# Down-projection steps behind half products, and exponentials in pieces, in a one-core encoder layer

## The chip, the cores and the metric

The kernel is one launch on one core of a Trainium2 chip. The metric is the time of the launch on the device in microseconds (us). Three runs of the kernel before took 2942.41, 2954.04 and 2954.80 us; the median is 2954.04 us. The names of the engines are those of the profile: PE is the matrix engine, PEld its weight loads, DVE the vector engine, ACT the engine for activation functions, POOL the general one, SP the one that issues all DMAs here.

## What is computed

One encoder layer on 2048 tokens of width 1024 in fp32: three mixers side by side (A: an attention that keeps 256 keys for each query, chosen by an index score; B: gated linear attention in chunks of 64; C: attention in a window), an output projection, and a gated feed-forward part (FFN) with 2816 inner columns.

```python
h = rms_norm(x, norm_mix[l])
p = h @ w_in[l]
out_a = dsa_mixer(q_a, c_kv, q_idx, k_idx, w_idx, kv_norm[l], w_uk[l], w_uv[l], rel_bias)
out_b = gla_mixer(q_b, k_b, v_b, g_lr, r_b, w_gate2[l], b_gate[l], gla_norm[l])
out_c = swa_mixer(q_c, k_c, v_c, sinks[l], rel_bias)
x = x + jnp.concatenate([out_a, out_b, out_c], axis=-1) @ w_out[l]
h = rms_norm(x, norm_ffn[l])
x = x + (jax.nn.silu(h @ w_ffn_gate[l]) * (h @ w_ffn_up[l])) @ w_ffn_down[l]
return rms_norm(x, final_norm)
```

In mixer A a block of 128 queries scores all earlier keys, keeps 256 (`lax.top_k`), adds a bias to their logits, takes a softmax and sums the values.

## The kernel before

Activations lie transposed, 128 channels on the partitions and 512 tokens (a group) along a row; there are four groups. Every dense product is made of two parts for each operand (`hi`, and `lo`, the rest), as three matmuls of 512 columns for each 128 rows of the contraction: a product with 8 such rows is 24 matmuls, and half of it (`FINE = 4` rows) is 12.

Two threads of work run at the same time on the one core, written as Python generators. The dense thread, `dense`, goes through the input projections (`pass1`), mixers B and C (`pass2`), and then the output projection and FFN (`ffn`) of groups 0 and 1. The other thread, `dsa`, goes through the 16 query blocks of mixer A: `select` of a block runs beside `attend` of the block ahead of it. `merge` takes a step of the thread that is behind by its share: each `yield` gives the cost of the step just written, in units of its author's, and the totals stand at the `merge` call (`FFN1`, `select_cost`, `attend_cost`, `SPEED`). The steps come out as one program, and a scheduler then moves single instructions ahead where their inputs and buffers allow, so that the final order on each engine is that of the `order` listings below. After both threads are done, `last` runs the output projection and FFN of groups 2 and 3 alone (`ffn` with two halves).

`select` finds the 256th largest score by bisection: 32 probes over the whole row, in turns on ACT (L935) and DVE (L937), each of which gives a count, and two short DVE instructions between them (L960, L962) that set the next threshold. Then a scan and masks (L983 to L990) make the mask `mk`. `attend` computes logits by strips on PE (L1030 to L1032), masks them and takes the extreme on DVE (L1034), takes one exponential per head over the whole row on ACT (L1038), turns 128x128 pieces on PE (L1047), copies them out of PSUM on ACT (L1049) and sums values on PE (L1057).

In `ffn`, `gate_up(f)` makes one of 22 inner tiles: the gate product, a tanh on ACT (L277) and a DVE instruction (L278), the up product, a DVE instruction (L283, tile `u`), and its split into `fh` and `fl` (ACT L116, POOL L119). `down(fs, ...)` adds two inner tiles to the output: eight steps (one for each output tile `oc`), each of six matmuls (L299 to L301) and an add to `x2` on DVE (L302; the profile writes `x`). In groups 0 and 1 the order is `gate_up(f)`, then all eight steps of `down([f - 2, f - 1])`, then `gate_up(f + 1)`. Products and steps take their PSUM bank in turn from the three of `mf`. `norm_scale` (L202) and `finish` (L324, L326) close a group.

Weights come 128x512 at a time into `w`, a ring of `N_W` buffers. Group 0 loads each from the input (`raw`), splits it on ACT (L116) and POOL (L119) and stores the two parts; later groups load the stored parts (L131). The rings of `w` and of `fh`/`fl` before, and the order of the inner loop:

```python
N_RAW, N_W, N_ACT = 3, 5, 3
...
for f in range(0, NF, 2):
    yield from gate_up(f)
    if f and n_act < 4:
        yield from down([f - 2, f - 1], steps)
    yield from gate_up(f + 1)
```

Of the kernel before, what the change touches and what calls it, by code (L numbers as in the profile page):

```python
# [1 line left out]

# [17 lines left out]
P = 128  # L20
# [57 lines left out]

N_RAW, N_W, N_ACT = 3, 5, 3
A_RAW, A_W = 3, 5  # L80
# [4 lines left out]
def hybrid_encoder_kernel(ctx, tc, xT, w_in, w_out, w_g, w_u, w_d, vec, wuk, wuv, wg2,  # L85
# [73 lines left out]

    def ffn(groups, pools, ps_f, ps_n, n_raw, n_w, n_act, n_lead, before):  # L160

# [7 lines left out]

        def product(ps, w, act, ks=range(KC), first=True, last=True):  # L170

            for k in ks:
                hi, lo = w[k // 4]
                a, b = (t[:, (k % 4) * P:(k % 4 + 1) * P] for t in (hi, lo))
                T.matmul(ps, a, act[k][0], start=(first and k == ks[0]), stop=False)  # L175
                T.matmul(ps, b, act[k][0], start=False, stop=False)  # L176
                T.matmul(ps, a, act[k][1], start=False, stop=(last and k == ks[-1]))  # L177
                if k % FINE == FINE - 1 and k < ks[-1]:
                    yield 0.65 * FINE


# [38 lines left out]
        def normed(i):  # L220

            hs = halves[i]
            norm_scale(hs)
            h2.append([])
            for k in range(KC):
                h2[i].append(operand(i, k))
                hi, lo = h2[i][k]
                hf = fr.tile([P, 512], F32, tag="m", bufs=3, name="hf")
                V.scalar_tensor_tensor(out=hf, in0=x2[:, k, hs], scalar=vc[:, V_FFN + k:V_FFN + k + 1],
                                       in1=rs[:, hs], op0=ALU.mult, op1=ALU.mult)  # L230
                A.copy(hi, hf)  # L231
                (V if k % 2 else Q).tensor_sub(lo, hf, hi.bitcast(F32))
                yield 0.4
# [31 lines left out]

        def gate_up(f):
            ah = ft.tile([P, W], F32R, tag="fh", bufs=n_act, name="fh")
# [4 lines left out]
            for i, hs in enumerate(halves):  # L272
                pg = ps_f()
                yield from product(pg, wg_, h2[i])

                s = ft.tile([P, 512], F32, tag="s", bufs=2, name="s")
                A.activation(s, pg, AF.Tanh, scale=0.5)  # L277
                V.scalar_tensor_tensor(out=s, in0=s, scalar=1.0, in1=pg, op0=ALU.add, op1=ALU.mult)  # L278
                yield 5.2 - 0.65 * (KC - FINE)
                pu = ps_f()  # L280
                yield from product(pu, wu_, h2[i])
                u = ft.tile([P, 512], F32, tag="u", bufs=2, name="u")
                V.scalar_tensor_tensor(out=u, in0=s, scalar=0.5, in1=pu, op0=ALU.mult, op1=ALU.mult)  # L283
                split(u, ah[:, hs], al[:, hs])
                yield 5.2 - 0.65 * (KC - FINE)

        def down(fs, parts, last=False):

            n, ws = len(fs), {}
            for i2, hs in parts:  # L290
                if i2 not in ws:
                    ws[i2] = [load_w(w_d, f, i2) for f in fs]
                for oc in range(i2 * 4, i2 * 4 + 4):
                    os_ = slice((oc % 4) * P, (oc % 4 + 1) * P)
                    ps = ps_f()[:, 0:hs.stop - hs.start]
                    for j, f in enumerate(fs):
# [41 lines left out]
        for f in range(0, NF, 2):  # L338
            yield from gate_up(f)
            if f and n_act < 4:  # L340
                yield from down([f - 2, f - 1], steps)
            yield from gate_up(f + 1)
            if f and n_act >= 4:
                yield from down([f - 2, f - 1], steps)
        yield from down([NF - 2, NF - 1], tail, True)
# [5 lines left out]
    with ExitStack() as mx:  # L351
# [648 lines left out]
        def attend(qb, res):  # L1000
# [15 lines left out]
            far = nk - nw  # L1016
            sl = strips(far) + [(far, nw)]
            den = sp.tile([P, 4], F32, tag="dena", name="dena")
            po = ps_o()

            def logits(hd):
# [5 lines left out]
                for si, (k0, w) in enumerate(sl):  # L1027
# [9 lines left out]
                    yield 0.9 * w / 512.0  # L1037
                A.activation(lg[:, 0:nk], lg[:, 0:nk], AF.Exp, scale=-1.0, bias=least[:, si:si + 1],  # L1038
                             accum_out=den[:, hd:hd + 1])

# [22 lines left out]
            for h2 in (0, 2):  # L1063
                yield from logits(h2)
                yield from logits(h2 + 1)
                for k4 in range(0, qb + 1, 4):
                    nxt = [turned(h2, k4)]
                    if wait:
                        summed(*wait)
                    nxt.append(turned(h2 + 1, k4))  # L1070
                    wait = nxt
                    yield 2.0 * nxt[0][2] / 4.0
            V.reciprocal(den, den)

# [3 lines left out]
            V.tensor_copy(dT, pt[0:4, 0:P])  # L1078
            summed(*wait)
            pb = ps_tr()  # L1080
            for hd in range(4):
# [10 lines left out]
        def attend_cost(qb):  # L1092
            return (qb + 1) * (0.9 + 1.0) + 1.5

# [24 lines left out]
        def dense():  # L1119
# [9 lines left out]
            with ExitStack() as f1:  # L1129
# [5 lines left out]
                for g in range(2):  # L1135
                    while len(attended) < 4 * g + 4:
                        yield None
                    end = yield from ffn([g], pools, lambda: mf.tile([P, 512], F32, tag="mf", name="mf"), ps_tr,
                                         N_RAW, N_W, N_ACT, 2, end)
# [5 lines left out]
    with ExitStack() as f2:  # L1145
# [6 lines left out]
        def last():  # L1152
            end = yield from ffn([2, 3], pools, lambda: pp.tile([P, 512], F32, tag="pf", name="pf"),
                                 lambda: pr.tile([P, 512], F32, tag="pm", name="pm"), 3, 9, 4, 6, iter(()))
# [93 lines left out]
```

## Time and profile before

| what | before |
|---|---|
| median of 3 runs | 2954.04 us |
| profiled execution, its own time | 2950.48 us |
| its span, first to last instruction | 2948.7 us |
| outside the span | 1.8 us |
| PE busy | 2761.6 us, 94% of the span |
| DVE, ACT, POOL busy | 57%, 40%, 20% |
| mean granted TensorE clock | 0.973 |
| chain that ended last | PE 59%, DVE 19%, ACT 8%, issue 7%, DMA 4% |

The table is read like this: PE is the engine that is busy nearly all of the time, so what counts is where it stands still and where it runs at the lower clock. A busy PE is not PE at its peak: a matmul of 512 columns is shown as 0.39 us long, while the next one starts 0.23 us after it. The profiled execution is 3.6 us faster than the median and 8.1 us slower than the fastest run.

The stages by time: projections and mixers B and C to about 970 us, the FFN of group 0 to about 1540 us, that of group 1 to 2083 us, the end of mixer A to 2103 us, and groups 2 and 3 to the end.

### The profile page before, as it was taken

The page shows a single profiled execution, that of the slowest core. Times are in us where ns is not written, and L with a number is a line of the kernel's source. Part 1 is how long each engine was busy: PE and PEld are TensorE (multiplying, and loading weights), DVE is VectorE, ACT ScalarE, POOL GpSimd, SP SyncE. Part 2 cuts the span into 40 slices and gives each one's busy share as a digit, 9 for nine tenths or more (in the row PEclk, how much of TensorE's full clock was granted, in tenths as well). Part 3 has the DMA queues.
Part 4 walks back from the last instruction along what each step waited for, and adds up shares of the span by engine and source line. Part 5 has one row for each costly group of instructions (what it writes and reads, how often), then busy time and mean ns, then how long its engine had stood idle before and what let it go on. Part 6 is the DMA issues. An engine that isn't in the chain of part 4 may idle for free.

```text
span 2948.7 us, 36635 instructions
## 1 busy us (share of the span) xinstructions
PE 2761.6 (94%) x13372; PEld 2171.4 (74%) x13372; DVE 1677.2 (57%) x3567; ACT 1181.1 (40%) x2061; POOL 582.8 (20%) x497
## 2 busy tenths in 40 slices
PE   7898999999999899999989999999899999999997
PEld 5666767676776767777767777777677888888886
DVE  3787887788767867475576673673342222222226
ACT  4655664665546655354553431441341000000004
POOL 3113420010100544444431100001111000000002
PEclk9998999999999989999999999999999999999998
DMA  7665534243332756666655444444572323323222
GB/s 248 193 190 191 183 122 142 92 149 106 103 128 78 268 179 229 227 214 225 226 187 193 142 150 143 137 152 147 188 249 87 108 92 100 100 86 107 93 93 72
DMA packets 179300, 451.12 MB, mean 153 GB/s; under 512 B 18632, under 2 KB 50288, under 8 KB 179120
## 3 DMA queue, kind: packets, MB, share of 16 engines
q1 hardware_dynamic: 179120, 448.78, 46.1%
q8 instruction: 105, 1.72, 0.2%
q14 instruction: 75, 0.61, 0.1%
HBM read 325.88 MB, written 122.83 MB: 152 GB/s over the span
## 4 chain that ended last, share of the span: by engine, by line
PE 59%; DVE 19%; ACT 8%; issue 7%; DMA 4%; POOL 2%; SPq 0%; DVEq 0%; ACTq 0%; POOLq 0%
PE pf L175 6%; PE pf L177 6%; PE pf L176 6%; DVE jd L937 6%; ACT jd L935 4%; PE mf L177 4%; PE mf L175 4%; PE mf L176 4%; PE pf L301 2%; PE pf L300 2%; PE pf L299 2%; PE mm L507 2%; PE mm L506 2%; PE mm L508 2%; PE mf L299 2%
## 5 line engine op out<-in xcount | busy, mean ns | idle before, releaser
L935 ACT ACTIVATE jd<-x,c 128x384 bf16<-128x384 f32 (+13 forms) x224 | 292.8, 1307 | 288.5 <-DVE c L962 228.7
L177 PE MATMUL mf<-al,w 128*128 128x512 f32 x832 | 329.1, 396 | 8.3 <-DVE al L212 4.1
L175 PE MATMUL mf<-ah,w 128*128 128x512 f32 x832 | 331.5, 399 | 3.7 <-ACT ah L231 2.8
L937 DVE TENSOR_SCALAR_CACHE_REDUCE jd<-x,c 128x384 bf16<-128x384 f32 (+13 forms) x224 | 330.9, 1477 | 6.5 <-DVE c L946 0.5
L175 PE MATMUL pf<-ah,w 128*128 128x512 f32 x832 | 325.1, 391 | 6.2 <-DMA w<-w 4.5
L119 POOL TENSOR_TENSOR w<-raw,w 128x512 fp32r<-128x512 f32 x192 | 260.0, 1362 | 341.4 <-ACT w L116 297.0
L176 PE MATMUL mf<-ah,w 128*128 128x512 f32 x832 | 327.4, 395 | 0.0
L177 PE MATMUL pf<-al,w 128*128 128x512 f32 x832 | 324.8, 391 | 1.3 <-POOL al L212 0.6
L176 PE MATMUL pf<-ah,w 128*128 128x512 f32 x832 | 325.3, 391 | 0.0
L119 POOL TENSOR_TENSOR fl<-u,fh 128x512 fp32r<-128x512 f32 x88 | 114.2, 1298 | 948.5 <-ACT fh L116 948.4
L506 PE MATMUL mm<-hh,w 128*128 128x512 f32 x576 | 241.3, 419 | 4.3 <-issue 2.0
L507 PE MATMUL mm<-hh,w 128*128 128x512 f32 x576 | 232.2, 403 | 0.6 <-POOL w L119 0.6
L508 PE MATMUL mm<-hl,w 128*128 128x512 f32 x576 | 230.9, 401 | 0.0
L177 PEld LDWEIGHTS mf<-al,w 128*128 128x128 f32 x832 | 158.5, 191 | 46.4 <-DVE al L212 4.5
L175 PEld LDWEIGHTS mf<-ah,w 128*128 128x128 f32 x832 | 159.0, 191 | 38.4 <-ACT ah L231 3.4
L175 PEld LDWEIGHTS pf<-ah,w 128*128 128x128 f32 x832 | 156.9, 189 | 39.9 <-DMA w<-w 4.9
L302 DVE TENSOR_TENSOR x<-x,pf 128x512 f32<-128x512 f32 (+1 forms) x184 | 121.9, 663 | 110.3 <-PE pf L301 110.0
L177 PEld LDWEIGHTS pf<-al,w 128*128 128x128 f32 x832 | 156.8, 188 | 35.9 <-POOL al L212 1.0
L176 PEld LDWEIGHTS mf<-ah,w 128*128 128x128 f32 x832 | 158.5, 190 | 31.7
L176 PEld LDWEIGHTS pf<-ah,w 128*128 128x128 f32 x832 | 156.8, 188 | 32.8 <-issue 0.5
L116 ACT CAST fh<-u 128x512 fp32r<-128x512 f32 x88 | 54.6, 620 | 308.1 <-DVE u L283 307.6
L299 PE MATMUL mf<-fh,w 128*128 128x512 f32 x352 | 147.0, 418 | 32.7 <-DVE x L302 17.3
(256 smaller groups left out, 5473.1 us busy)
## 6 DMA issues: line engine op xcount, KB each, us to landing
w<-w SPq DMA_DIRECT2D x636, 512.0 KB, 3.5
xk<-in_xT_dram SPq DMA_DIRECT2D x64, 256.0 KB, 3.3
raw<-in_w_in_dram SPq DMA_DIRECT2D x44, 256.0 KB, 3.7
raw<-in_w_g_dram SPq DMA_DIRECT2D x44, 256.0 KB, 3.7
raw<-in_w_u_dram SPq DMA_DIRECT2D x44, 256.0 KB, 3.9
raw<-in_w_d_dram SPq DMA_DIRECT2D x44, 256.0 KB, 4.3
m<-mixT SPq DMA_DIRECT2D x32, 256.0 KB, 3.1
x<-in_xT_dram SPq DMA_DIRECT2D x32, 256.0 KB, 4.6
```

The costliest lines, as they stand in the source:

```text
L119: Q.tensor_sub(lo, src, hi.bitcast(F32))
L175: T.matmul(ps, a, act[k][0], start=(first and k == ks[0]), stop=False)
L176: T.matmul(ps, b, act[k][0], start=False, stop=False)
L177: T.matmul(ps, a, act[k][1], start=False, stop=(last and k == ks[-1]))
L299: T.matmul(ps, hi[:, os_], ah[:, hs], start=(j == 0), stop=False)
L300: T.matmul(ps, lo[:, os_], ah[:, hs], start=False, stop=False)
L302: V.tensor_add(x2[:, oc, hs], x2[:, oc, hs], ps)
L506: T.matmul(ps, a, hh, start=(k == 0), stop=False)
L507: T.matmul(ps, b, hh, start=False, stop=False)
L508: T.matmul(ps, a, hl, start=False, stop=(k == KC - 1))
L935: A.activation(jd, xs, AF.Sign, scale=-1.0, bias=c[:, 0:1], accum_out=cnt)
L937: V.tensor_scalar(out=jd, in0=xs, scalar1=c[:, 0:1], scalar2=0.0, op0=ALU.is_ge, op1=ALU.add, accum_out=cnt)
```

## The change

- The down steps of groups 0 and 1 are no longer in one run of eight. `product` takes a generator `beside` and takes one step of it after its first half; `gate_up` takes one after each product. So a step of six matmuls stands behind each half product of twelve, and the eight steps of two tiles are spread over two `gate_up`.
- These steps have a PSUM bank of their own (`md`, one buffer); gate and up products keep two (`mf`). Groups 2 and 3 are as before.
- The ring of `w` has 7 buffers instead of 5, that of `fh` and `fl` 4 instead of 3.
- The exponential of a head is taken in pieces of 512 columns, each with its own sum in `dens`; the sums are added on DVE before the reciprocal.
- `attend` yields at five more kinds of places (5.0 units in all for a block), so that dense work may be written there, and `attend_cost` grows by 5.0. `normed` yields 3.0 before the norm.

```diff
-N_RAW, N_W, N_ACT = 3, 5, 3
+N_RAW, N_W, N_ACT = 3, 7, 4
...
                 if k % FINE == FINE - 1 and k < ks[-1]:
                     yield 0.65 * FINE
+                    yield from islice(beside, 1)
...
             hs = halves[i]
+            yield 3.0
             norm_scale(hs)
...
-                yield from product(pg, wg_, h2[i])
+                yield from product(pg, wg_, h2[i], beside=beside)
...
                 yield 5.2 - 0.65 * (KC - FINE)
+                yield from islice(beside, 1)
...
-                    ps = ps_f()[:, 0:hs.stop - hs.start]
+                    ps = ps_d()[:, 0:hs.stop - hs.start]
...
-            yield from gate_up(f)
-            if f and n_act < 4:
-                yield from down([f - 2, f - 1], steps)
-            yield from gate_up(f + 1)
-            if f and n_act >= 4:
-                yield from down([f - 2, f - 1], steps)
+            last_two = down([f - 2, f - 1], steps) if f else iter(())
+            for f_ in (f, f + 1):
+                yield from gate_up(f_, last_two if nh == 1 else iter(()))
+            yield from last_two
...
+            n4 = (nk + 511) // 512
+            dens = sp.tile([P, 4, 4], F32, tag="dens", name="dens")
...
-                A.activation(lg[:, 0:nk], lg[:, 0:nk], AF.Exp, scale=-1.0, bias=least[:, si:si + 1],
-                             accum_out=den[:, hd:hd + 1])
+                for j, k0 in enumerate(range(0, nk, 512)):
+                    e = lg[:, k0:min(k0 + 512, nk)]
+                    A.activation(e, e, AF.Exp, scale=-1.0, bias=least[:, si:si + 1],
+                                 accum_out=dens[:, hd, j:j + 1])
+                yield 0.5
...
+                    if k4 == 0:
+                        yield 1.0
...
-            V.reciprocal(den, den)
+            if n4 > 1:
+                V.tensor_reduce(out=den, in_=dens[:, :, 0:n4], axis=AX.X, op=ALU.add)
+                V.reciprocal(den, den)
+            else:
+                V.reciprocal(den, dens[:, :, 0])
+            yield 0.5
...
             summed(*wait)
+            yield 0.5
...
-            return (qb + 1) * (0.9 + 1.0) + 1.5
+            return (qb + 1) * (0.9 + 1.0) + 6.5
...
-                mf = f1.enter_context(tc.tile_pool(name="mf", bufs=3, space=PSUM))
...
-                    end = yield from ffn([g], pools, lambda: mf.tile([P, 512], F32, tag="mf", name="mf"), ps_tr,
+                    end = yield from ffn([g], pools, lambda: mf.tile([P, 512], F32, tag="mf", bufs=2, name="mf"),
+                                         lambda: mf.tile([P, 512], F32, tag="md", bufs=1, name="md"), ps_tr,
```

The change in the order of instructions is shown at three places. First DVE in the FFN of group 1, beside the probes of the last query block (2048 columns). `jd,cnt<-x,c` is a probe, `up` and `c` set the next threshold, `s` and `u` take a gate and an up product out of PSUM, and `x_...<-x_...,mf` is the add of a down step. Before:

```order
L960 TENSOR_SCALAR up<-cnt,nth,ps_16671 128x1
L962 TENSOR_SCALAR c<-c,st,up 128x1
L937 TENSOR_SCALAR jd,cnt<-x,c 128x2048
L283 SCALAR_TENSOR_TENSOR u<-s,mf 128x512
L960 TENSOR_SCALAR up<-cnt,kp,ps_16671 128x1
L962 TENSOR_SCALAR c<-c,st,up 128x1
L302 TENSOR_TENSOR x_14013<-x_14013,mf 128x512 x2
L960 TENSOR_SCALAR up<-cnt,nth,ps_16671 128x1
L962 TENSOR_SCALAR c<-c,st,up 128x1
L937 TENSOR_SCALAR jd,cnt<-x,c 128x2048
L302 TENSOR_TENSOR x_14013<-x_14013,mf 128x512 x2
```

The same place now, with the line numbers of the changed file:

```order
L941 TENSOR_SCALAR jd,cnt<-x,c 128x2048
L308 TENSOR_TENSOR x_13931<-x_13931,md 128x512
L964 TENSOR_SCALAR up<-cnt,kp,ps_17170 128x1
L966 TENSOR_SCALAR c<-c,st,up 128x1
L964 TENSOR_SCALAR up<-cnt,nth,ps_17170 128x1
L966 TENSOR_SCALAR c<-c,st,up 128x1
L308 TENSOR_TENSOR x_13931<-x_13931,md 128x512
L941 TENSOR_SCALAR jd,cnt<-x,c 128x2048
L964 TENSOR_SCALAR up<-cnt,kp,ps_17170 128x1
L966 TENSOR_SCALAR c<-c,st,up 128x1
L288 SCALAR_TENSOR_TENSOR u<-s,mf 128x512
```

Adds in pairs behind a probe have become single adds, about one for each DVE probe, each with a bank `md` behind it.

Second ACT at the end of the `attend` that runs beside the last `select` (`fh` is a split, `s` a tanh, `pT` a copy out of PSUM). Before:

```order
L976 ACTIVATE jd,cnt<-x,ntt,sg 128x2048
L116 CAST fh<-u 128x512
L1038 ACTIVATE big,dena<-big,least 128x1920
L277 ACTIVATE s<-mf 128x512
L1049 COPY pT<-tr 128x512 x2
L116 CAST fh<-u 128x512
```

The same stretch of the block ahead of it, now:

```order
L980 ACTIVATE jd,cnt<-x,ntt,sg 128x1920
L281 ACTIVATE s<-mf 128x512
L1046 ACTIVATE big,dens<-big,least 128x512 x3
L1046 ACTIVATE big,dens<-big,least 128x256
L1058 COPY pT<-tr 128x512
L117 CAST fh<-u 128x512
```

One exponential has become four in a row.

Third DVE at the end of group 1, where mixer A ends too (`dT`, `ma` and `ll` are short steps of `attend`, `big,least<-sc,...` is a strip of logits, `rs` the sum of squares of the last norm, L326 and L332 its `finish`). Before:

```order
L1078 COPY dT<-tr 4x128
L1087 TENSOR_TENSOR ma<-o,bs 128x256
L302 TENSOR_TENSOR x_14013<-x_14013,mf 128x512 x8
L1013 SCALAR_TENSOR_TENSOR ll<-sc,lh 128x512
L1034 ISA big,least<-sc,mk 128x512
L1034 ISA least 128x1
L1034 ISA big,least<-sc,mk,least 128x512
L1034 ISA least 128x1
L278 SCALAR_TENSOR_TENSOR s<-s,mf 128x512
```

Now:

```order
L308 TENSOR_TENSOR x_13931<-x_13931,md 128x512
L199 TENSOR_TENSOR rs<-rs,sq 128x512
L332 SCALAR_TENSOR_TENSOR x_13931<-x_13931,vc,rs 128x512 x5
L1094 COPY dT<-tr 4x128
L1104 TENSOR_TENSOR ma<-o,bs 128x256
L1017 SCALAR_TENSOR_TENSOR ll<-sc,lh 128x512
L1040 ISA big,least<-sc,mk 128x512
L1040 ISA least 128x1
```

The `attend` of the last block stood beside the last products and steps of group 1 (84 matmuls come on PE after its first one); now it stands behind the end of the group, with no dense work beside it.

## Rows read from the trace of the kernel before

**Rows 1.** Windows by stage: us, PE, PEld, DVE, ACT, POOL busy, clock, DMA.

```profile
970.00:1540.00 570.00, 527.34 (x2527) 418.24 (x2525) 368.07 (x693) 299.54 (x461) 257.31 (x199) 0.96 0.64 219
1540.00:2040.00 500.00, 469.99 (x2287) 377.42 (x2288) 299.53 (x530) 174.16 (x232) 43.38 (x40) 0.97 0.48 155
2104.00:2949.00 845.00, 816.32 (x3610) 673.57 (x3608) 251.79 (x363) 119.30 (x192) 94.44 (x74) 0.99 0.35 116
```

**Rows 2.** Waits of PE from 0 to 2104 us: total, times, longest.

```profile
PE mf L299 <- DVE x L302: 17.3, 11, 3.4
...
PE mf L299 <- DVE u L283: 12.0, 6, 4.5
...
PE tr L1082 <- DVE dT L1078: 5.4, 3, 3.1
...
PE mf L299 <- ACT fh L116: 2.7, 1, 2.7
```

**Rows 3.** PE groups, 970 to 2104 us: busy, mean ns, idle before, releaser.

```profile
L1047 PE MATMUL tr<-cs,big 128*128 128x128 f32 x344 | 56.1, 286 | 17.2 <-ACT big L1038 15.8 <-ACT rs L148 1.3
L1057 PE MATMUL o<-pT,cv 128*64 128x128 f32 x688 | 53.3, 285 | 9.0 <-ACT pT L1049 9.0
```

**Rows 4.** Timeline of PE at 1902 us, a down step's start.

```profile
1902.50 0.39 PE L300 MATMUL mf<-fh,w 128*128 128x512 f32 x1
1902.73 0.39 PE L301 MATMUL mf<-fl,w 128*128 128x512 f32 x1
1907.65 0.79 PE L299 MATMUL mf<-fh,w 128*128 128x512 f32 x1 [4.54 <-DVE u L283]
```

**Rows 5.** Timeline of DVE in the same stretch.

```profile
1898.90 2.34 DVE L937 TENSOR_SCALAR_CACHE_REDUCE jd<-x,c 128x2048 bf16<-128x2048 f32 x1
...
1904.03 0.27 DVE L960 TENSOR_SCALAR up<-cnt,nth,ps 128x1 f32<-128x1 f32 x1 [2.16 <-ACT jd L935]
...
1904.64 2.35 DVE L937 TENSOR_SCALAR_CACHE_REDUCE jd<-x,c 128x2048 bf16<-128x2048 f32 x1
...
1906.91 0.68 DVE L283 SCALAR_TENSOR_TENSOR u<-s,mf 128x512 f32<-128x512 f32 x1
```

**Rows 6.** Windows of 20 us with a low granted clock (column before the last two).

```profile
1720.00:1740.00 20.00, 15.09 (x52) 11.21 (x51) 15.48 (x32) 6.96 (x8) 1.26 (x1) 0.83 0.32 100
...
1900.00:1920.00 20.00, 15.46 (x71) 12.19 (x70) 14.56 (x25) 7.86 (x9) 1.29 (x1) 0.83 0.28 90
```

**Rows 7.** Line L302: ns min/median/max, first and last start.

```profile
L302 DVE TENSOR_TENSOR x<-x,mf x176: 655/684/691, 1090.9 to 2080.5; 128x512 f32<-128x512 f32 x176
```

**Rows 8.** Line L131, 1600 to 2040 us: reloads of weights, issue to landing.

```profile
DMA to landing us min/median/max: 3.3/3.5/5.3
```

**Rows 9.** Groups of 970 to 1540 us: the two splits of a weight.

```profile
L119 POOL TENSOR_TENSOR w<-raw,w 128x512 fp32r<-128x512 f32 x146 | 198.1, 1366 | 243.1 <-ACT w L116 208.5 <-DMA w<-w 7.0 <-DMA raw<-in_w_g_dram 6.3
...
L116 ACT CAST w<-raw 128x512 fp32r<-128x512 f32 x145 | 87.8, 615 | 88.2 <-PE mf L177 37.2 <-PE mf L301 19.0 <-issue 13.6
```

**Rows 10.** ACT groups by form: the exponentials' total and mean ns.

```profile
L1038 ACT ACTIVATION_READ_ACCUMULATOR big<-big,least 128x1 f32 x64 | 11.9, 186 | 0.0
...
L1038 ACT ACTIVATE big<-big,least 128x1920 f32<-128x1920 f32 x4 | 7.6, 1900 | 9.4 <-DVE least L1034 9.4
...
L1038 ACT ACTIVATE big<-big,least 128x512 f32<-128x512 f32 x4 | 2.9, 720 | 4.2 <-DVE least L1034 4.2
```

**Rows 11.** Timeline of DVE at the last scan, and at the close of group 1.

```profile
1981.97 4.42 DVE L985 TENSOR_TENSOR_SCAN x<-ones,mk 128x2048 f32<-128x2048 f32 x1
...
2088.88 6.54 DVE L326 SCALAR_TENSOR_TENSOR x<-x,vc,rs 128x512 f32<-128x512 f32 x5
```

**Rows 12.** Windows of 20 us at the end of mixer A.

```profile
2060.00:2080.00 20.00, 19.45 (x130) 15.22 (x130) 9.80 (x18) 12.81 (x21) 1.92 (x2) 1.00 0.00 1
2080.00:2100.00 20.00, 17.46 (x124) 12.68 (x122) 13.29 (x26) 12.32 (x16) 4.62 (x3) 0.91 0.40 145
```

**Rows 13.** Waits of PE, 2040 to 2200 us: the longest one.

```profile
PE pf L175 <- DMA w<-w: 4.5, 1, 4.5
```

More of the change, by code (lines that the diff above doesn't have):

```diff
@@ L1 @@
 from contextlib import ExitStack
+from itertools import islice
 import numpy as np
@@ L157, in sigmoid, with ffn @@
         A.activation(dst, dst, AF.Exp)
-    def ffn(groups, pools, ps_f, ps_n, n_raw, n_w, n_act, n_lead, before):
+    def ffn(groups, pools, ps_f, ps_d, ps_n, n_raw, n_w, n_act, n_lead, before):
         fx, ft, fh, fl, fo, fs, fr = pools
@@ L168, in load_w, with product @@
             return load_halves((src.tensor.name, f, c), src[f][:, c * 512:(c + 1) * 512], fr, n_raw, fh, n_w)
-        def product(ps, w, act, ks=range(KC), first=True, last=True):
+        def product(ps, w, act, ks=range(KC), first=True, last=True, beside=iter(())):
             for k in ks:
@@ L264, in ffn, with gate_up @@
             yield from normed(i)
-        def gate_up(f):
+        def gate_up(f, beside=iter(())):
             ah = ft.tile([P, W], F32R, tag="fh", bufs=n_act, name="fh")
@@ L279, in gate_up @@
                 yield 5.2 - 0.65 * (KC - FINE)
+                yield from islice(beside, 1)
                 pu = ps_f()
-                yield from product(pu, wu_, h2[i])
+                yield from product(pu, wu_, h2[i], beside=beside)
                 u = ft.tile([P, 512], F32, tag="u", bufs=2, name="u")
@@ L285, in gate_up @@
                 yield 5.2 - 0.65 * (KC - FINE)
+                yield from islice(beside, 1)
         def down(fs, parts, last=False):
@@ L1152, in last @@
         def last():
-            end = yield from ffn([2, 3], pools, lambda: pp.tile([P, 512], F32, tag="pf", name="pf"),
+            ps_f = lambda: pp.tile([P, 512], F32, tag="pf", name="pf")
+            end = yield from ffn([2, 3], pools, ps_f, ps_f,
                                  lambda: pr.tile([P, 512], F32, tag="pm", name="pm"), 3, 9, 4, 6, iter(()))
```

## The prediction

> **What bounds the kernel now.** First I read the windows by stage, to see where PE, the engine that is busy 94% of the span, stands still. In the last 845 us (groups 2 and 3 alone) PE is busy 816 of 845 us at a clock of 0.99, and the change leaves this stage as it is [rows 1]. What it moves lies ahead of 2104 us, most of all in the two FFN stages from 970 to 2040 us: there PE is idle 43 and 30 us, and the clock of 0.96 and 0.97 stands for 23 and 15 us more at full speed (570 x 0.04, 500 x 0.03) [rows 1]. The waits of PE say what the idle time is: 32.0 us before the first matmul of a down step (L299), which waits for its PSUM bank: 17.3 us for the adds of earlier steps, 12.0 us for `u`, which still reads a product's bank, and 2.7 us for `fh` [rows 2]; 15.8 us before transposes that wait for an exponential, and 9.0 us before value sums that wait for a copy by ACT [rows 3]. Then I read one such wait on both engines. PE has finished a step and stands from 1903 to 1907.65 for `u` [rows 4]. DVE had nothing long of its own to do for `u`: 0.68 us. But `u` was queued behind a threshold update that waited 2.16 us for a probe on ACT, and behind the next probe of 2.35 us [rows 5]. Behind such waits the clock falls: the window from 1900 to 1920 us has 0.83, so 6.8 us at the lower level (1.2 GHz of 2.4), which costs 3.4 us of work [rows 6]. Four windows are like this behind waits of L299 or L1047 (two stand in the rows), which makes 13.6 us, and some smaller dips beside them 5 us: about 19 us of the 38.
>
> So the stage is held by two things that lock together: PE, and the chain of probes, whose cycle on the last block is at least 5.74 us (from 1898.90 to 1904.64) [rows 5]. I take the sum against the profiled execution: 2950.5 us (span 2948.7 us and 1.8 us around it), 3.6 us under the median of 2954.0 us.
>
> **The change part by part.**
>
> *Own bank, steps apart.* A step no longer shares a bank with `u`, and the next product of the same bank comes two products later. The 12.0 us go, and the 2.7 us with them, since `fh` of the last tile has a down step and a half product (18 matmuls x 0.227 us [rows 4] = 4.1 us) for a cast of 0.62 us and a subtraction of 1.3 us: **-14.7 us**. The 17.3 us of adds are less sure. Before, a step waits for the add three steps back, so two steps (12 matmuls, 2.7 us) lie between; now it waits for the add one step back, with a half product (12 matmuls, 2.7 us) between. The room is the same. What is better is that adds of 0.68 us [rows 7] no longer come every 1.36 us in runs of eight. The delay that one probe and one wait for ACT make (2.35 + 2.16 us, [rows 5]) is longer than 2.7 us in both orders. I take **-5 us**, with ends at -17.3 (all gone) and +17.3 (twice as often).
>
> The Trainium skill (Perfetto Trace Analysis, section Optimizing Tensor Performance, Matmuls) says that independent groups of matmuls should rotate through different PSUM banks, so that the evacuation of one overlaps the next. That speaks against one bank for all steps. The trace of before, with three, waits 17.3 us all the same [rows 2]; by the rule this term would be positive, and the second rival below prices that from rows.
>
> *The closing runs.* After the last tile of a group, eight steps still come in a row, now on one bank: each waits for the add ahead of it, 0.68 us [rows 7] and some 0.2 us for the signals (an estimate from the 0.23 us pace), seven times: **+6 us** for group 0. Group 1's run is in the tail below.
>
> *Exponentials in pieces.* A transpose that waits for the whole row (1.90 us) waits for 0.72 us instead, and dense steps are written in between [rows 10]. Of the 15.8 us I take **-10 us** (ends -15.8 and 0); the 9.0 us for copies stay. The two new yields near the reciprocal put work before the wait for `dT`: **-4 us** of 5.4 [rows 2]. The price lies on ACT: 64 exponentials become 160 instructions. From 720 ns at 512 and 1900 ns at 1920 columns a piece costs 0.29 us before its first column, and 0.19 us to read its sum [rows 10]: 96 x 0.48 = 46 us on ACT, which is about half busy in these stages [rows 1]. It counts only where a probe stands behind it: **+3 us**, ends 0 and +25.
>
> *Clock.* The waits taken away are 29.7 of 47.8 us (32.0 + 15.8), 62%; the same share of 19 us is **-12 us** (ends -19 and 0).
>
> *Weights of the down steps.* The ring grows to 7, but a pair of down weights now takes its buffers late: seven loads earlier stands the second up weight of the tile before, whose last matmul comes one step and a half product ahead of the use, so 18 matmuls or 4.1 us, and a little attention work. Counted in the order of before with its ring of 5, no load has less than 30 matmuls (6.8 us). A reload lands 3.3 to 5.3 us after its issue, 3.5 us in the middle [rows 8]; in group 0 cast and subtraction take 0.62 + 1.37 us, and the second subtraction stands behind the first [rows 9]. So most are just in time. For the 40 pairs that stand beside products I take 0.2 us each, **+9 us**; the ends are 0 and +60 (1.5 us each).
>
> *The tail.* The thread of mixer A now has 80 units more to go, so it falls behind the dense thread. Before, 84 matmuls (19 us) lie beside the last `attend`; now none, and DVE closes group 1 before it: scan 4.42 us, finish 6.54 us [rows 11], nine adds and seven sums at 0.68 us, masks and small ones some 5 us, together 27 us against about 19 us of PE work: 8 us. The last `attend` without cover shows its price in the second half of that of before: from 2083 to 2103 us, where the clock drops to 0.91 and PE has waits, PE loses about 8 us, and the window ahead, with cover, loses 0.6 [rows 12]. Now the first half does too. Together **+16 us**, ends 8 and 30. In return the first weights of groups 2 and 3 are issued while the last `attend` runs, so of the wait of 4.5 us [rows 13] I take **-4 us**.
>
> The sum: -14.7 - 5 + 6 - 10 - 4 + 3 - 12 + 9 + 16 - 4 = -15.7 us. 2950.5 - 15.7 = **2935 us**.
>
> **The rivals.**
>
> *The stalls come back on one bank, no change.* In the probe phases there is now one add for each DVE probe, so PE walks in step with the probe chain: a step and a half product are 4.1 us, a cycle 5.74 us [rows 5]. If one step in ten of the 160 waits 2 us more, the adds' term is +10 instead of -5, and the clock gives back 4 instead of 12: 2935 + 15 + 8 = 2958 us, within 0.5%. For it: the wait at 1902 us is just such a delay. Against it: PE also waits less often for the other reasons.
>
> *Down weights late, slower.* Each pair lands 1.5 us too late because the load, or the split on ACT behind a probe of 2.0 us, starts when its buffer falls free: 60 us instead of 9, 2986 us. It decides from about 1.1 us a pair (2935 - 9 + 43 = 2969 us). For it: 4.1 us of lead against up to 5.3 us to landing [rows 8]. Against it: attention work between them adds to the lead.
>
> *All stalls go, faster.* Adds never stall (-17.3), exponentials never (-15.8), the whole 19 us of clock returns: 2935 - 12.3 - 5.8 - 7 = 2910 us. Against it: the cycle of 5.74 us is a floor that no bank changes.
>
> That the steps are not where the code writes them is ruled out by the order on DVE, which has them apart.
>
> **How the numbers follow.** 0.5% of the median, about what a measurement of this kernel can tell from no change, is 14.8 us: faster ends at 2939 us, slower begins at 2969 us. Forecast (2922 to 2948 us, by half the ends of its unsure terms) 0.45; no change on one bank 0.25; weights late 0.14; all stalls gone 0.16. Faster is 0.16 and three quarters of the forecast's 0.45, so 0.50; slower is 0.14 and the upper end of the second case, 0.03, so 0.17; the rest, 0.33, is the same. The range reaches from under the fast case, with its unsure tail, to the edge of the slow one: 2900 to 2970 us. It leaves out most of the case of late weights and little else.
>
> **What would show it.** No wait of a down step for `u`; waits for the adds on `md` between 5 and 20 us; the transposes' wait for the exponential under 8 us; few windows under 0.85 in the FFN stages; PE waiting for `w` in down steps under 15 us; a stretch of some 60 us before groups 2 and 3 with PE at two thirds; the last stage at 845 us as before. The prediction is wrong if waits for `md` or for down weights pass 40 us, or if the tail costs over 30 us.

## The result

| | before | changed |
|---|---|---|
| median of 6 runs each | 2951.34 us | 2972.30 us |
| all runs | 2942.41 to 2954.80 | 2966.19 to 2977.81 |
| profiled execution | 2950.48 us | 2966.19 us |
| mean granted clock | 0.973 | 0.977 |

The ratio is 1.0074, with a 95% interval of 1.0054 to 1.0094: slower by 0.7%, where 2935 us was forecast, and 2 us past the upper end of the range. The profiled execution of the changed kernel is its fastest run, 6.1 us under its median; the two traces differ by 15.7 us.

The windows of the changed kernel by stage come first (columns as in [rows 1]): group 0, group 1 to its last down step, the stretch from there to the first product of groups 2 and 3, and these two groups.

```profile
948.00:1503.00 555.00, 514.25 (x2461) 406.72 (x2460) 344.73 (x674) 289.78 (x498) 240.71 (x192) 0.97 0.63 219
1503.00:2056.00 553.00, 506.87 (x2432) 398.90 (x2433) 352.20 (x630) 218.20 (x339) 54.05 (x46) 0.98 0.45 146
2056.00:2122.00 66.00, 51.10 (x352) 37.03 (x350) 24.69 (x55) 31.40 (x67) 7.88 (x7) 0.87 0.34 121
2122.00:2964.00 842.00, 818.12 (x3610) 674.84 (x3610) 252.66 (x364) 119.48 (x193) 95.32 (x74) 0.98 0.34 111
```

The third of these stretches is this one in the kernel before:

```profile
2079.00:2103.00 24.00, 21.00 (x152) 15.09 (x151) 15.78 (x31) 15.36 (x22) 6.30 (x5) 0.93 0.40 143
```

So the last stage is 3 us shorter (842 for 845 us), and everything ahead of it takes 19 us more: it starts at 2122.6 us, before at 2103.6. The third stretch has grown by 42 us and holds 200 more instructions of PE, 30 us of its busy time; part of that busy time is at the lower clock, and the granted clock of the stretch fell from 0.93 to 0.87. Worked out with the usual spacing of each kind of matmul (0.23 us for 512 columns), about 14 us of the 42 is work that only moved there, and 28 us is loss. So all that lies ahead of this stretch gave back 9 us (2079.5 us before; 2056.6 and the 14 us afterwards).

Why only 9? These are the waits of PE from 945 to 2125 us in the changed kernel (total, times, longest), to be laid beside [rows 2, 3]:

```profile
PE md L305 <- DVE x L308: 38.5, 33, 4.6
PE sc L1036 <- DVE least L1040: 10.9, 5, 4.3
PE md L306 <- POOL w L120: 7.7, 9, 1.6
PE tr L204 <- DVE rs L199: 7.4, 2, 5.2
...
PE md L305 <- ACT w L117: 2.4, 3, 1.4
...
PE md L305 <- ACT fh L117: 2.1, 2, 1.3
...
PE md L305 <- DMA w<-w: 1.9, 3, 0.9
...
PE tr L1056 <- ACT big L1046: 1.2, 1, 1.2
```

The wait of the strips of logits before, in the same window:

```profile
PE sc L1030 <- DVE least L1034: 1.9, 4, 1.2
```

No down step waits for `u` any more, and the transposes, which waited 15.8 us for exponentials [rows 3], wait 1.2 us. But steps wait 38.5 us for adds, in 33 places, where it was 17.3 us in 11 [rows 2]; strips of logits (L1036), which waited 1.9 us for DVE before, wait 10.9 us; and the sums that close a group (`rs`), for which PE waited 0.9 us before, hold it for 7.4 us, 5.2 of them at the end of group 0. All waits of PE in this window add up to 102 us, before to 81. Here is one wait for an add, on PE: the end of a step, the last matmul of the half product behind it, and the start of the next step.

```profile
1757.96 0.40 PE L307 MATMUL md<-fl,w 128*128 128x512 f32 x1
...
1760.69 0.39 PE L178 MATMUL mf<-al,w 128*128 128x512 f32 x1
...
1762.64 0.50 PE L305 MATMUL md<-fh,w 128*128 128x512 f32 x1 [1.57 <-DVE x L308]
```

And on DVE in the same stretch:

```profile
1759.15 2.21 DVE L941 TENSOR_SCALAR_CACHE_REDUCE jd<-x,c 128x1920 bf16<-128x1920 f32 x1
...
1761.41 0.27 DVE L964 TENSOR_SCALAR up<-cnt,kp,ps 128x1 f32<-128x1 f32 x1
1761.72 0.27 DVE L966 TENSOR_SCALAR c<-c,st,up 128x1 f32<-128x1 f32 x1
1761.91 0.68 DVE L308 TENSOR_TENSOR x<-x,md 128x512 f32<-128x512 f32 x1
```

The step is done at 1758.36 (1757.96 and 0.40). Its add stands in DVE's queue behind a probe of 2.21 us and the threshold updates on either side of it, so it runs at 1761.91, and the next step, which has nowhere else to write, starts 1.57 us late.

### The profile page after: what moved, and what is told of

Same layout as the page of the kernel before. It is cut to its first block, busy times and chain, and to the rows that moved or that the text cites. A ratio compares the mean times of both kernels' runs of the same rounds, so it can differ in the third digit from the quotient of the medians.

```text
span 2964.4 us, 36825 instructions
## 1 busy us (share of the span) xinstructions
PE 2762.6 (93%) x13372; PEld 2162.9 (73%) x13372; DVE 1680.3 (57%) x3579; ACT 1206.2 (41%) x2253; POOL 578.9 (20%) x497
## 4 chain that ended last, share of the span: by engine, by line
PE 55%; DVE 17%; ACT 8%; issue 6%; DMA 2%; POOL 2%; SPq 0%; ACTq 0%; DVEq 0%; POOLq 0%
PE pf L178 6%; PE pf L177 6%; PE pf L176 6%; DVE jd L941 5%; ACT jd L939 4%; PE mf L178 4%; PE mf L176 4%; PE mf L177 3%; PE pf L306 2%; PE pf L305 2%; PE pf L307 2%; PE md L305 2%; PE md L306 2%; PE md L307 2%; PE o L1066 1%
## 5 line engine op out<-in xcount | busy, mean ns | idle before, releaser
L510 PE MATMUL mm<-hh,w 128*128 128x512 f32 x576 | 237.0, 412 | 4.9 <-DVE qe L656 1.8
L511 PE MATMUL mm<-hh,w 128*128 128x512 f32 x576 | 229.1, 398 | 0.3 <-POOL w L120 0.3
L308 DVE TENSOR_TENSOR x<-x,md 128x512 f32<-128x512 f32 x176 | 120.2, 683 | 123.9 <-PE md L307 123.4
L305 PE MATMUL md<-fh,w 128*128 128x512 f32 x352 | 147.8, 420 | 45.0 <-DVE x L308 38.5
L176 PEld LDWEIGHTS pf<-ah,w 128*128 128x128 f32 x832 | 156.9, 189 | 35.4 <-issue 1.5
```

What stands on the lines that cost most here:

```text
L305: T.matmul(ps, hi[:, os_], ah[:, hs], start=(j == 0), stop=False)
L308: V.tensor_add(x2[:, oc, hs], x2[:, oc, hs], ps)
L510: T.matmul(ps, a, hh, start=(k == 0), stop=False)
L511: T.matmul(ps, b, hh, start=False, stop=False)
```

## Experiments

Each ratio is against the kernel before, run beside it on the same chip, with its 95% interval. Times in us from a difference of ratios are for 2950 us. Waits of PE are from 945 to 2125 us, in one execution of each kernel; those executions lie between 9 us under the median of their kernel (e10) and 7 us over it (e9), so a few us between single waits prove little.

**e1: the tail covered.** The changed kernel with

```diff
-SPEED = 1.3
+SPEED = 1.35
```

> The changed kernel with one number altered: the weight of the attention thread in the merge goes from 1.3 to 1.35, so that 54 matmuls of the FFN lie beside the last attend, where the changed kernel has none and the kernel before had 84. Everything else is as in the changed kernel. In the two traces the stretch from the last down step of group 1 to the first product of groups 2 and 3 is 24 us before and 66 us after, and some 14 us of the 42 us more is work that only moved there. Theory (the bare last attend costs the other 28 us): the stretch shrinks to 25 to 40 us, the clock in it is back above 0.9, and the time is 2972 - 20 = about 2952 us (2945 to 2960). Rival (the chain of probes on ACT and DVE ends last and would only push the idle time elsewhere): the idle time comes back before the last attend, as waits of PE in the last select, and the time stays at 2966 to 2978 us.

Measured: 2956.82 us, ratio 1.0031 (1.0019 to 1.0043). The stretch to the first product of groups 2 and 3 is 38 us instead of 66:

```profile
2073.00:2111.00 38.00, 29.03 (x204) 21.36 (x202) 16.51 (x33) 19.53 (x39) 6.43 (x5) 0.87 0.56 201
```

The theory holds, with the clock as a miss: it stays at 0.87. From 1.0074 to 1.0031 is 13 us. The waits for adds are 30.9 us in 26 places.

**e2: the own bank undone.** The changed kernel with

```diff
-... tag="mf", bufs=2, name="mf"),
-    lambda: mf.tile([P, 512], F32, tag="md", bufs=1, name="md"), ps_tr,
+... tag="mf", bufs=3, name="mf"),
+    lambda: mf.tile([P, 512], F32, tag="mf", bufs=3, name="mf"), ps_tr,
```

> The changed kernel with the own bank undone alone: half products and down steps take turns in three banks, as before; the steps still go one behind each half product. Theory (a step waits for the add of the step ahead because this add stands in DVE's queue behind a probe, and the one bank makes every such delay a wait of PE: 38.5 us): with three banks the wait for adds falls below 10 us, but a product now takes the bank that the product ahead has just finished, with one down step (1.4 us) in between, so products wait for s and u by at least as much; PE's waits in the two FFN stages are as large or larger, 2970 to 3000 us. Rival (the one bank alone makes the loss, and rotation would cure it): waits for adds go and nothing takes their place, 2940 to 2955 us.

Measured: 2951.74 us, ratio 1.0017 (1.0007 to 1.0027). The theory fell and the rival's time stands, though not all waits for adds go. Waits of PE for a bank, by what it waits for (adds, `u` and `s`):

```profile
PE mf L176 <- DVE x L308: 14.0, 8, 3.2
...
PE mf L305 <- DVE x L308: 5.5, 4, 2.4
...
PE mf L305 <- DVE u L288: 4.3, 3, 1.9
...
PE mf L305 <- DVE s L282: 1.8, 5, 0.4
```

The 38.5 us for adds became 14.0 us before products and 5.5 us before steps; `u` and `s` came back with 6.1 us only. From 1.0074 to 1.0017 is 17 us for one bank. Whether the loss lies in the bank being apart or in its being a single one was not tried: a pair for the steps would have left the products one of the three. This is the rule that the prediction weighed and set aside, that of the Trainium skill (Perfetto Trace Analysis, section Optimizing Tensor Performance, Matmuls): independent groups rotate through different banks. The trace agrees with it here: 25.6 us of waits for banks with three in turns, 38.5 us with one apart.

**e3: the dense half alone.** The kernel before with the changes to `product`, `gate_up`, `down`, `ffn`, the banks and the rings; `attend` as before.

> The dense half of the change alone: down steps one behind each half product on a bank of their own, rings of 7 and 4; the exponentials, the yields and the cost of attend are as in the kernel before. 108 matmuls of the FFN lie beside the last attend, so its tail is covered. Theory (own bank: waits for u gone, 12 us, waits for adds up by 21 us, clock and first weights back some 12 us; the tail belongs to the other half): waits for adds stay at 30 to 40 us, waits of transposes for the exponential come back at 14 to 17 us, and the time is level with the kernel before, 2945 to 2960 us. Rival (the dense half alone makes the loss): 2965 to 2980 us.

Measured: 2952.73 us, ratio 1.0016 (1.0007 to 1.0026), as the theory said. Waits for adds and for exponentials:

```profile
PE md L305 <- DVE x L308: 35.3, 28, 2.7
...
PE tr L1051 <- ACT big L1042: 6.4, 7, 1.4
```

One part of the expectation missed: with whole rows and no new yields the transposes wait 6.4 us, not 14 to 17. That steps which stand apart already come between an exponential and its transposes is the likely reason; it is argued, not tried.

**e4: the attention half alone.** The kernel before with the changes to `attend` and `attend_cost`.

> The attention half of the change alone: exponentials in pieces of 512, the new yields, the cost of attend up by 5 a block; the down steps stand in runs of eight in three banks, rings of 5 and 3, as before. No matmul of the FFN lies beside the last attend. Theory (the tail comes from this half and costs 28 us, the exponentials' wait of 15 us goes): the stretch from the last down step of group 1 to the first product of groups 2 and 3 is 60 to 70 us, waits for u (12 us) and adds (17 us) stand as in the kernel before, and the time is 2955 to 2970 us. Rival (the attention half gains what it was priced at and the loss is the dense half's alone): 2935 to 2945 us.

Measured: 2955.69 us, ratio 1.0036 (1.0023 to 1.0050): this half loses too, as the theory said, and its tail is bare. Waits for adds, which were to stand at 17 us, are 25.8 us. The stretch:

```profile
2041.00:2112.00 71.00, 52.99 (x372) 37.92 (x370) 33.18 (x64) 32.95 (x69) 9.37 (x9) 0.86 0.31 113
```

**e5 to e8: both cures, each half cured, and the tail by itself.** e5 is e2 with `SPEED = 1.36`; e6 is e3 with e2's edit; e7 is e4 with `SPEED = 1.36`; e8 is the kernel before with `SPEED = 1.25`.

> The changed kernel with both losses taken away: half products and down steps take turns in three banks (as in e2), and the attention thread's weight is 1.36, so that 102 matmuls of the FFN lie beside the last attend. Theory (the one bank and the bare tail are two separate losses: e2 gave back 20 us and e1 15 us): 2972 - 35 = 2937 us (2930 to 2943), faster than the kernel before. Rival (both cures lift the same idle time, since PE waits for the probe chain in either case): no better than e2 alone, 2948 to 2954 us.

Measured: 2937.34 us, ratio 0.9961 (0.9948 to 0.9974). The two losses add up; the table below has the account.

> The dense half of the change alone (as e3, tail covered by 108 matmuls), but with the own bank undone: three banks in turns. Theory (the one bank costs the 35 us of waits for adds that e3 shows, of which some 15 to 20 are given back): waits for adds, in front of steps and products together, fall to about 20 us, and the time is 2953 - 18 = 2935 us (2930 to 2943). Rival (the gain of e2 came from the attention half's yields, which lie between the steps there, and isn't to be had without them): 2948 to 2955 us.

Measured: 2931.59 us, ratio 0.9941 (0.9928 to 0.9955). Against e3 the bank is worth 0.75%, 22 us. Some of the waits that remain in it, the longest but one first:

```profile
PE tr L1051 <- ACT big L1042: 7.3, 6, 1.9
PE mf L176 <- DVE x L308: 7.3, 7, 2.5
PE mf L306 <- POOL w L120: 7.3, 8, 1.6
PE mf L305 <- DVE s L282: 7.3, 6, 2.2
PE mf L305 <- DVE u L288: 5.2, 4, 2.4
...
PE mf L305 <- ACT w L117: 3.0, 4, 1.7
...
PE mf L305 <- DVE x L308: 0.3, 1, 0.3
```

Adds make 7.6 us (7.3 and 0.3), where the theory had 20, and `s` and `u` 12.5 us: 20 us together, where e3 had 35.

> The attention half of the change alone (as e4), with the attention thread's weight at 1.36, so that 72 matmuls of the FFN lie beside the last attend. Theory (e4 lost its gain in the bare tail): the stretch from the last down step of group 1 to the first product of groups 2 and 3, 71 us in e4, shrinks to 30 to 45 us, and the time is 2956 - 18 = 2938 us (2932 to 2945). Rival (pieces of the exponential bring nothing: what the transposes waited is now waited for in front of steps and strips, 26 and 7 us in e4): 2946 to 2955 us.

Measured: 2932.03 us, ratio 0.9943 (0.9930 to 0.9957), and the stretch is half of that of e4:

```profile
2051.00:2087.00 36.00, 27.71 (x186) 20.51 (x185) 17.66 (x34) 18.98 (x37) 7.22 (x5) 0.86 0.47 170
```

> The kernel before with one number altered: the weight of the attention thread is 1.25 instead of 1.3, so that no matmul of the FFN lies beside the last attend (255 matmuls behind the last dense one, 247 in the changed kernel). It prices the bare tail without any other part of the change. Theory (the bare tail costs 15 to 28 us by itself): 2948 + 20 = 2968 us (2960 to 2976). Rival (the last attend got dear through the pieces and yields, not through its missing cover): 2946 to 2953 us.

Measured: 2971.30 us, ratio 1.0066 (1.0054 to 1.0079): as slow as the changed kernel, from one number. Its stretch:

```profile
2060.00:2124.00 64.00, 50.54 (x368) 36.11 (x366) 26.20 (x58) 29.23 (x44) 7.99 (x7) 0.92 0.33 124
```

The number also shifts attention work elsewhere (steps wait 22.3 us for `u` in e8, 12.0 before), so not all of the 19 us is the tail's. The other three pairs give it as 13 us (changed kernel to e1), 17 us (e2 to e5) and 27 us (e4 to e7), and in them, too, the number moves other waits: those of the strips from 10.9 to 4.6 us in the first, those for adds from 25.8 to 12.5 us in the last.

**e9, e10 and e12: pieces or yields.** e9 is e5 with the exponentials over whole rows again; e10 is e6 with the pieces added, and no new yields; e12 is e7 with whole rows. The edit, in e9 and e12 as shown and in e10 the other way:

```diff
-for j, k0 in enumerate(range(0, nk, 512)):
-    e = lg[:, k0:min(k0 + 512, nk)]
-    A.activation(e, e, AF.Exp, ..., accum_out=dens[:, hd, j:j + 1])
+A.activation(lg[:, 0:nk], lg[:, 0:nk], AF.Exp, ..., accum_out=den[:, hd:hd + 1])
 yield 0.5
```

> e5 with one thing undone: each head's exponential again runs over the whole row in one instruction, while the yields and the cost of attend stay as in the changed kernel. e5 is at 2937 us, but each half alone is at 2932 us (e6, e7), so together they give 13 us where the sum would be 37. Theory (the pieces cost ACT, and so the probes, what they save the transposes; the yields alone are the gain): 2926 to 2936 us, with waits of transposes for the exponential back at 5 to 10 us. Rival (the pieces are worth their instructions, the halves collide elsewhere): 2940 to 2950 us.

Measured: 2936.19 us, ratio 0.9963 (0.9951 to 0.9975), beside 0.9961 with pieces. Neither side is borne out: the pieces move no time that can be told from nothing, and the collision of the halves is not theirs.

> e6 (dense half, three banks in turns, tail covered) with the exponentials in pieces added and nothing else of the attention half: no new yields, the cost of attend as before. With e5, e6 and e9 it makes the four cases of pieces and yields. Theory (pieces alone save the 7 us that transposes wait for the exponential in e6 and cost about as much on ACT): 2928 to 2936 us. Rival (pieces are the gain of the attention half): 2915 to 2926 us.

Measured: 2934.70 us, ratio 0.9951 (0.9934 to 0.9967), beside 0.9941 without pieces. Two of its waits move in opposite directions:

```profile
PE mf L305 <- ACT w L117: 7.1, 5, 2.3
...
PE tr L1055 <- ACT big L1046: 3.3, 4, 1.5
```

The exponentials' wait falls from 7.3 to 3.3 us, and the wait for ACT's cast of a down weight rises from 3.0 to 7.1 us. That the one became the other along ACT's queue is not shown. In the pair e9 and e5 all waits for down weights fall with the pieces, from 18.8 us (11.1 POOL, 5.9 DMA, 1.8 ACT) to 13.3 us (8.1, 3.0, 2.2).

> e7 without the pieces: the kernel before with only the new yields and the cost of attend, tail covered by 72 matmuls, exponentials over whole rows. e7 is at 2932 us, 18 under the kernel before; e9 and e10 moved less than their intervals by the pieces. Theory (the yields, which put FFN work between the parts of attend, are the gain of the attention half): 2928 to 2938 us, and the wait of transposes for the exponential, 15.8 us in the kernel before, falls below 8 us although the rows stay whole. Rival (without the dense half the pieces matter, since no step stands beside the exponentials): 2942 to 2952 us.

Measured: 2935.71 us, ratio 0.9949 (0.9935 to 0.9963), beside 0.9943 with pieces. So the attention half has its gain without the pieces: the yields and the weight of 1.36 make it. How much the weight alone gives was not tried (the kernel before with 1.36 was not run). Transposes wait for whole rows 3.0 us, 15.8 before:

```profile
PE tr L1048 <- ACT big L1038: 3.0, 3, 1.6
```

**e11: one buffer more for weights.** e6 with

```diff
-N_RAW, N_W, N_ACT = 3, 7, 4
+N_RAW, N_W, N_ACT = 3, 8, 4
```

> e6 with the ring of weights at 8 instead of 7, so that a load takes the buffer of a weight one earlier. In e6 PE waits 12 us for down weights in front of steps (7.3 for the subtraction on POOL, 3.0 for the cast on ACT, 1.7 for the DMA). Theory (the lead of a half product and a step is what is short): these waits fall to 4 us or less, 2920 to 2928 us. Rival (the lead is set by the three raw buffers and the splits behind one another on POOL, not by the ring): waits and time as in e6, 2929 to 2936 us.

Measured: 2929.14 us, ratio 0.9936 (0.9920 to 0.9951), the fastest of all. The three waits for down weights, 12.0 us in e6, come down to one row:

```profile
PE mf L306 <- POOL w L120: 1.3, 1, 1.3
```

The lead was what they waited for, but the theory's time (2920 to 2928 us) was missed: the ratio moves by 0.05%, inside both intervals. The 10.7 us of waits that are gone are answered by others (exponentials 10.7 us instead of 7.3, `u` 7.6 instead of 5.2, adds 11.4 instead of 7.6); all waits of PE add up to 71 us in e6 and 72 us in e11.

| kernel | bank of the steps | tail | ratio to before |
|---|---|---|---|
| changed | own, one | bare | 1.0074 |
| e1 | own, one | covered | 1.0031 |
| e2 | three, in turns | bare | 1.0017 |
| e5 | three, in turns | covered | 0.9961 |
| e3, dense half | own, one | covered | 1.0016 |
| e6, dense half | three, in turns | covered | 0.9941 |
| e4, attention half | as before | bare | 1.0036 |
| e7, attention half | as before | covered | 0.9943 |

The first four rows make the account. Without both losses the change is worth -0.39% (-11.5 us). The bank costs 17 us with the tail bare and 21 us with it covered (0.57% and 0.70%; the second pair differs also by 1.35 and 1.36 in `SPEED`), the bare tail 13 us with one bank and 17 us with three (0.43% and 0.56%). In either order the three add up to the +0.74% (+22 us) that was measured, as four ratios must. What the rows do show is that each loss costs the same, within 0.13% (4 us), whether the other is there or not; that is inside the intervals.

## Why the prediction was wrong

**The step that failed** is the adds' term in "Own bank, steps apart". It took -5 us, with ends at -17.3 and +17.3; the waits for adds went from 17.3 to 38.5 us. Of the 38.5 us, 6.5 us in 7 places lie in the closing run of group 1, which the prediction counts under the tail, and 1.0 us in 2 places in that of group 0, for which it had +6. The other 31.0 us, in 24 places, make this term +14 instead of -5. In time, the one bank costs 17 to 22 us against banks in turns (three pairs).

The working said that "the room is the same", 2.7 us from an add's start of waiting to the next use of its bank. That is right for one step, and the wait at 1760 us shows it. What it left out is how many steps meet that room alone. Before, steps stood in runs of eight: only a delay of DVE that fell into a run met a step, in 11 places. Afterwards each of the 176 steps has one bank and 2.7 us, beside a chain of probes that holds DVE for 2.2 us at a time: 33 places. With the steps as far apart and three banks, it is 12 places (e2). The rival "the stalls come back on one bank" had the mechanism and even this picture (PE in step with the probe chain). Its price, one step in ten of the 160 waiting 2 us more, was near: 24 of them wait, 1.3 us each, which is +14 where it had +10. And the rule of rotation spoke for it. The prediction set that rule aside because three banks waited too; but a rule that speaks of fewer waits isn't met by the finding that some remain.

**The tail** was seen, and its sign was right, but by the trace this term was too small as well: +16 us (8 to 30) against 28 us in the stretch, with the 6.5 us of the closing run on top. Changing `SPEED` gives 13 to 17 us back in time, and it moves other waits as well (e8). The 5.2 us for `rs` at the end of group 0 stood in no term. Why the thread of mixer A fell behind stands in the code: its total at the `merge` call is `SPEED` times the sum, over the blocks, of the larger of `select_cost` and `attend_cost`, and `attend_cost` is the larger in the first two blocks alone. So of the 80 new units only 10 enter that sum, while all 80 count as work done. Going from 1.3 to 1.36 adds 61 units to the total, nearly what is missing.

One wait in the tail was not foreseen; PE at the last `attend`, for its queries:

```profile
2075.55 2.07 PE L1012 MATMUL sc<-qa,wuk_s 128*128 128x128 f32 x8 [4.35 <-DMA qa<-qaD]
```

With dense work beside it nobody had to wait for that load: e1, e5 and e7 have no such wait, and e2, e4 and e8, whose tails are bare, have 3.9, 4.1 and 3.8 us.

**Exponentials.** The waits fell even further than forecast (15.8 to 1.2 us, where 10 were to go), but the pieces aren't needed for it: e12 has 3.0 us with whole rows. Adding or removing the pieces moves no time that can be told (0.9961 and 0.9963, 0.9951 and 0.9941, 0.9943 and 0.9949, with pieces first). The price on ACT was right in kind. The groups of ACT by form:

```profile
L1046 ACT ACTIVATE big<-big,least 128x512 f32<-128x512 f32 x112 | 79.8, 714 | 52.7 <-DVE least L1040 52.7
...
L1046 ACT ACTIVATION_READ_ACCUMULATOR big<-big,least 128x1 f32 x160 | 30.0, 187 | 0.0
...
L1046 ACT ACTIVATE big<-big,least 128x256 f32<-128x256 f32 x16 | 8.0, 498 | 0.0
```

The reads of sums alone went from 11.9 [rows 10] to 30.0 us. What it cost PE is open: the casts of down weights wait more with pieces in e10, less in e5. The strips (L1036) wait 9 us more than before; that this is the transposes' wait come back is not shown, and with the tail covered it is 4.6 us (e1).

**What went as forecast.** Waits for `u` went (12.0 to none); those for `fh` are 2.1 us instead of 2.7, so -12.6 of the -14.7 in waits. The wait for `dT` fell from 5.4 to 0.8 us, -4 forecast. Down weights: 12.0 us of waits in the changed kernel (7.7, 2.4, and 1.9 for the DMA), +9 forecast; that rival's price of 60 us was far off. The first weights of groups 2 and 3: -3 us, -4 forecast. The closing run of group 1 has steps 2.44 us apart, with 1.36 us of work; its first two waits are longer:

```profile
2040.20 0.50 PE L305 MATMUL md<-fh,w 128*128 128x512 f32 x1 [1.09 <-DVE x L308]
...
2043.38 0.50 PE L305 MATMUL md<-fh,w 128*128 128x512 f32 x1 [1.53 <-DVE x L308]
...
2050.70 0.50 PE L305 MATMUL md<-fh,w 128*128 128x512 f32 x1 [0.78 <-DVE x L308]
...
2053.14 0.50 PE L305 MATMUL md<-fh,w 128*128 128x512 f32 x1 [0.78 <-DVE x L308]
```

That is 1.08 us of loss a step, 0.9 forecast. In group 0 attention work stood between the steps, and its run waited 1.0 us for adds in all, where +6 was forecast.

**The clock.** Between the two traces the mean rose from 0.973 to 0.977, which is 12 us of 2950, the number forecast; the six runs of the changed kernel lie between 0.971 and 0.977. That the number came out is luck. It was to come from 29.7 us of waits taken away, and these waits (47.8 us for adds, `u`, `fh` and exponentials) fell by 6 us only, to 41.8. Two windows of 20 us with waits for adds, and one more:

```profile
1760.00:1780.00 20.00, 16.95 (x85) 12.90 (x83) 14.69 (x28) 7.49 (x10) 1.29 (x1) 1.00 0.43 133
...
1940.00:1960.00 20.00, 16.20 (x86) 12.51 (x84) 14.11 (x26) 8.63 (x11) 1.28 (x1) 1.00 0.43 142
...
1220.00:1240.00 20.00, 17.37 (x79) 14.06 (x80) 6.80 (x8) 3.98 (x7) 7.49 (x8) 0.83 0.42 142
```

In the first two PE is idle for 3.1 and 3.8 us, in waits of 0.5 to 2.3 us, and the clock stays at its upper level. The third has less idle time, 2.6 us, but it is the end of the longest wait for an add, and the clock falls behind it as it does in [rows 4, 6]:

```profile
1222.63 0.80 PE L305 MATMUL md<-fh,w 128*128 128x512 f32 x1 [4.58 <-DVE x L308]
```

But a long wait is not the only thing that goes before a fall, as the second of these windows of the tail shows:

```profile
2060.00:2080.00 20.00, 12.21 (x88) 8.65 (x87) 7.84 (x8) 6.45 (x11) 4.61 (x3) 0.79 0.88 307
...
2100.00:2120.00 20.00, 17.33 (x125) 12.96 (x123) 5.03 (x19) 10.72 (x26) 0.00 (x0) 0.83 0.01 1
```

In the first lies the wait of 4.35 us for the queries; in the second the longest waits are 1.2 and 1.5 us, among short transposes and value sums.

**What the sum missed beyond that.** Without the terms for adds and tail it comes to -27 us; e5, where both losses are gone, is at -11.5 us, and that with 9.7 us less of waits for adds than before. Some of its waits:

```profile
PE mf L306 <- POOL w L120: 8.1, 10, 1.5
...
PE mf L305 <- DVE s L282: 6.8, 6, 1.8
...
PE mf L307 <- POOL fl L120: 3.9, 7, 1.1
```

Down weights hold PE for 13.3 us there, where +9 was forecast. The waits for `s` (0.7 us before) and `fl` (1.2 before) were not in the sum. All waits of PE add up to 75 us in e5 and to 81 us before: most of what the change takes away is waited for elsewhere. No fixed rate of waits to time follows from these runs. In e11, 10.7 us of waits went and others took their place; in e2, all waits fell from 102 to 87 us, and the time by 17 us.

**What stays open.** Each half alone, with its loss cured, gives 17 us (e6, e7); together they give 11.5 us, not 34. They overlap: the dense half by itself halves the exponentials' wait (15.8 to 7.3 us in e6), and the attention half lowers the adds' (17.3 to 12.5 us in e7, 13.5 in e12). That may account for part of it; why both together are no faster than either (0.9961 against 0.9941 and 0.9943, a difference about as wide as the intervals) was not settled, only that the pieces have no visible part in it (e9). Nor is the gain of the dense half divided: its steps apart and its larger rings were not tried one without the other.

## What to carry to other kernels

When work is spread to fill gaps, count how many times its result has to be fetched out of its bank in time, and by which queue: a private bank with one buffer turns each delay of that queue into a wait, and the same banks taken in turns let most of the delay pass. When a change makes one of two merged threads longer, look at which of them ends last; here a merge weight that was off by 4% cost as much as the whole change could bring, because a cost was raised that the thread's total did not count. Credit a gain to an edit only when the edit has been tried alone: here the half with the pieces gained as much without them.

## What the runs showed of the hardware

PE idle for 3 to 4 us out of 20 did not lower the granted clock in the windows at 1760 and 1940 us (1.00), where it came in waits of 0.5 to 2.3 us. Behind one wait of 4.5 us, before and after the change, stand windows at 0.83. No rule follows: the window at 2100 us has 0.83 with 2.7 us idle and no wait over 1.5 us. Splitting one ACT instruction over 1920 columns into three of 512 and one of 256 made 1.90 us into 2.64 us (three times 0.714, and 0.498), so 0.25 us for each new piece, and a read of 0.19 us came with each. Summed over the kernel the reads went from 11.9 to 30.0 us of ACT, and no change of time showed in three pairs of runs.
